# A hybrid trunk layer on one core: the plan of the engines' order takes two engines' reads of one PSUM tile as ordered

## The chip, the cores and the metric

The kernel runs on one core of a Trainium2 chip. A core has a matmul engine (PE, TensorE), a vector engine (DVE), a scalar engine (ACT), a general one (POOL) and a queue that issues DMAs (SP). Each engine takes its instructions strictly in the order in which they stand in its own queue; between engines the order is kept by semaphores. PE writes to PSUM, a small buffer that DVE and ACT read. The metric is the device time of one execution in microseconds; lower is better.

## The reference

Two layers are computed for 640 tokens (512 latent tokens and 128 context tokens). In each layer one projection of the normalised input feeds three token mixers: attention with low-rank queries and keys over 8 heads (A), a chunked DeltaNet with 4 heads in both directions (B), and a chunked gated MLP (C). Cut to what matters:

```
def _layer(x, mod, p, cache=None):
    shift, scale, gate = split(mod, 3)
    proj = (rms(x, norm_g) * (1 + scale) + shift) @ w_in
    cq, ckv, krope, z_a, qkv_b, ga, gb, z_b, cu, cv, z_c, gl = split(proj)
    o_a = attend(q, k, v)            # softmax over context and latent keys
    o_b = rms(gdn(forward) + gdn(backward))
    o_c = chunk_mlp(cu, cv)
    br = stack(o_a * silu(z_a), o_b * silu(z_b), o_c * silu(z_c))
    yb = br @ w_branch               # one matrix per branch
    y = sum(sigmoid(gl) * yb) @ w_o
    return x + gate * y

def gdn_step(S, xs):                 # one chunk of DeltaNet, one head, one direction
    v_new = u - w @ S
    o = (q * exp(g)) @ S + att @ v_new
    S = S * exp(g_last) + (k * exp(g_last - g)).T @ v_new
```

## The kernel before, in words

Activations lie with channels on partitions and the 640 tokens along the free axis, in two halves of 320 columns. A projection is a sum over 8 channel blocks, and each f32 product is made of three matmuls on parts rounded to a short form (names `hi`, `lo`, `hh`, `hl`): 24 matmuls for one half, which PE writes into a PSUM tile of the tag `dn`. PSUM has three tags with two buffers each: `dn` (dense products), `mm` (one bank) and `p2` (two banks, shown as `p` in the profile).

The kernel's body doesn't emit instructions. It calls a recorder (class `Recorder`), which keeps every operation with the tiles that it reads and writes. For each operation `add` (line 115 on) goes through the earlier accesses of its tiles and makes an earlier operation a predecessor where one of the two writes and their ranges meet. For a PSUM tile the range is the whole tile (`box`). `plan` then runs a list schedule: each operation has a cost from a table, each engine takes the ready operation of the best priority, each tile has to find a free buffer of its tag, and a hop between engines costs a fixed number of ns. `best` plans four times, with 0, 60, 120 and 180 ns added to each hop that ends on PE (`SLACKS`), and keeps the plan whose modelled total is the least. `issue` emits the instructions in the order of that plan (line 371 is the one line that emits, so nearly every row of the profile has L371), and the framework below puts in the semaphores. In the emitted program two engines never read one PSUM tile at once: the one that stands second in the order of issue waits for the first.

The places with such pairs of reads, with the names that the profile shows:

- The scan of DeltaNet (`gdn_head`, line 1018 on). For each chunk and direction PE makes two products of the state into one tile `pks` (tag `mm`). DVE makes `rp` from its left part (`Q<-mm,g_nE,G`), which the rest of the step hangs on: PE multiplies it by the inverse (`mm<-Q,G`), ACT scales the result twice (`Q<-mm,res` and `V<-mm,br`), and PE makes from it the update of the state. From the right part of `pks` the output `z` is started, on ACT for the first of the two directions that reach a chunk (`V<-mm,g_E`) and on DVE for the second. There are 32 chunk steps in all whose `z` is on ACT (4 per head, 4 heads, 2 layers). In the recorded order `rp` comes ahead of `z`.
- The MLP's normalisation (in `layer`, after `gv`): five tiles per layer of tag `dn` are read by DVE's `bn_stats` and by ACT's copy (`D<-dn`).
- The low-rank projections (`lowrank`), the heads' preparation (`prep`) and the context part of attention (`context_tile`, with two softmaxes on one tile).

The scans of heads 0 to 3 and the preparation of attention run beside dense projections that the planner lays between them; after about 40% of a layer the attention stage runs beside the projections of branches A and C, and then come the branches' and the output's dense products.

Of the kernel before, what the change touches and what calls it, by code (L numbers as in the profile page):

```python
# [59 lines left out]
class Recorder:  # L60
# [57 lines left out]
    def add(self, eng, meth, args, kw):  # L118
        op = Op()
        op.n, op.eng, op.meth, op.args, op.kw = len(self.ops), eng, meth, args, kw  # L120
        op.prio = op.n - self.off
        op.preds, op.succs, op.tiles = set(), [], []
        outs, ins = [], []
        for i, x in enumerate(args):
            if isinstance(x, bass.AP):
                (outs if i == 0 else ins).append(x)
        for k, x in kw.items():
            if isinstance(x, bass.AP):
                (outs if k == "accum_out" else ins).append(x)
        for w, aps in ((False, ins), (True, outs)):  # L130
            for ap in aps:
                nm = ap.tensor.name
                if nm not in self.tag:
                    continue
                p0, p1, m = self.box(ap)
                lst = self.acc.setdefault(nm, [])
                keep = []
                for a_ in lst:
                    q, qw, q0, q1, qm = a_
                    hit = (w or qw) and q0 < p1 and p0 < q1 and (m & qm)  # L140
                    if hit and q is not op:
                        op.preds.add(q.n)
                    if not (w and p0 <= q0 and q1 <= p1 and (qm & ~m) == 0 and q is not op and q.eng != "SP"):
                        keep.append(a_)
                keep.append((op, w, p0, p1, m))
                self.acc[nm] = keep
                u = self.users.setdefault(nm, [])
                if not u or u[-1] is not op:
                    u.append(op)
                if nm not in op.tiles:  # L150
                    op.tiles.append(nm)
        self.cost(op, outs, ins)
        self.ops.append(op)
# [1656 lines left out]
```

## Time and profile before

| | us |
|---|---|
| median of 3 runs | 1702.54 (1701.52 to 1705.32) |
| the profiled execution's own time | 1704.07 |
| its span, from the first to the last instruction | 1702.3 |
| PE busy | 1646.9 (97%) |
| DVE busy | 1287.8 (76%) |
| ACT busy | 884.9 (52%) |

The profile is of one execution, whose time is 1.5 us above the median of the runs. PE is busy nearly throughout. A layer takes about 850 us, and the second shows nearly the same pattern as the first. What is below the span is PE's idle time, and it lies in few places: the start, the stretch with the DeltaNet heads in both layers, and the border between the layers.

### The profile page before, as it was taken

The numbers are of one execution on the slowest core, as the hardware profiler recorded it, in microseconds if no ns is written. First come the engines' busy times: TensorE is split into PE (matmuls) and PEld (weight loads), VectorE is DVE, ScalarE is ACT, GpSimd is POOL, SyncE is SP. The second block draws the span as 40 slices with busy tenths as digits, with TensorE's granted clock in tenths as the row PEclk, the third lists the DMA queues.
The fourth block names the chain that finished last, engine by engine and source line by source line (L and its number), as shares of the span: only waits on it lengthen the run. The fifth ranks groups of instructions, "written<-read, shape, count | busy, mean of one in ns | idle before, by whom it ended". The sixth has DMA issues, their size and how long they took to land.

```text
span 1702.3 us, 34983 instructions
## 1 busy us (share of the span) xinstructions
PE 1646.9 (97%) x13286; PEld 1538.8 (90%) x13286; DVE 1287.8 (76%) x3638; ACT 884.9 (52%) x2201; POOL 16.6 (1%) x100
## 2 busy tenths in 40 slices
PE   6999999999999999999999999999999999999998
PEld 5998988999888889999989989889988888899998
DVE  4898888565655777887987988885656557779898
ACT  3566665554544554444445676645545445545453
POOL 0000000000000000000000000000000000000000
PEclk9999999999999999999989999999999999999999
DMA  9311211221111213564542212112221122123252
GB/s 295 99 54 51 62 57 44 70 63 59 47 58 49 84 59 107 157 201 153 189 154 59 61 42 62 57 57 64 69 59 40 53 63 74 52 83 101 85 168 80
DMA packets 94617, 146.39 MB, mean 86 GB/s; under 512 B 14064, under 2 KB 38000, under 8 KB 94448
## 3 DMA queue, kind: packets, MB, share of 16 engines
q1 hardware_dynamic: 94448, 144.15, 27.5%
q8 instruction: 105, 1.72, 0.4%
q14 instruction: 64, 0.52, 0.1%
HBM read 132.28 MB, written 11.83 MB: 85 GB/s over the span
## 4 chain that ended last, share of the span: by engine, by line
PE 84%; DVE 8%; ACT 6%; issue 1%; DMA 0%; SPq 0%; DVEq 0%; ACTq 0%
PE dn L371 44%; PE p L371 24%; PE mm L371 16%; ACT iv L371 2%; DVE lo L371 1%; DVE iv L371 1%; DVE C L371 1%; ACT G L371 1%; DVE G L371 1%; ACT hi L371 1%; DVE ya L371 1%; ACT V L371 1%; DVE mx L371 1%; ACT C L371 1%; DVE D L371 0%
## 5 line engine op out<-in xcount | busy, mean ns | idle before, releaser
L371 PE MATMUL dn<-hh,hi 128*128 128x320 f32 (+1 forms) x1472 | 469.5, 319 | 7.7 <-ACT hh L371 4.2
L371 PE MATMUL dn<-hh,lo 128*128 128x320 f32 (+1 forms) x1472 | 470.8, 320 | 0.0
L371 PE MATMUL dn<-hl,hi 128*128 128x320 f32 (+1 forms) x1472 | 468.9, 319 | 0.0
L371 PEld LDWEIGHTS dn<-hh,hi 128*128 128x128 f32 (+1 forms) x1472 | 276.9, 188 | 14.6 <-ACT hh L371 5.6
L371 PEld LDWEIGHTS dn<-hl,hi 128*128 128x128 f32 (+1 forms) x1472 | 277.5, 189 | 5.1 <-issue 2.8
L371 PEld LDWEIGHTS dn<-hh,lo 128*128 128x128 f32 (+1 forms) x1472 | 277.5, 189 | 3.6 <-issue 1.8
L371 ACT CAST hi<-raw 128x512 fp32r<-128x512 f32 (+1 forms) x300 | 185.8, 619 | 179.0 <-PE dn L371 79.1
L371 DVE TENSOR_TENSOR lo<-raw,hi 128x512 fp32r<-128x512 f32 (+1 forms) x300 | 205.7, 686 | 66.6 <-ACT hi L371 61.5
L371 PE MATMUL dn<-qkv,hi 128*128 128x320 f32 x768 | 176.4, 313 | 0.0
L371 PEld LDWEIGHTS dn<-qkv,hi 128*128 128x128 f32 x768 | 129.8, 189 | 2.5 <-ACT hi L371 1.6
L371 PE MATMUL dn<-qkv,lo 128*128 128x320 f32 x384 | 120.1, 313 | 0.0
L371 ACT CAST hi<-D 128x512 fp32r<-128x512 f32 x88 | 54.6, 621 | 108.0 <-PE dn L371 55.4
L371 PE MATMUL p<-hh,hi 128*128 128x320 f32 x296 | 92.2, 312 | 0.6 <-ACT hi L371 0.6
L371 PE MATMUL p<-hl,hi 128*128 128x320 f32 x296 | 92.2, 312 | 0.2 <-DVE hl L371 0.2
L371 PE MATMUL p<-hh,lo 128*128 128x320 f32 x296 | 92.1, 311 | 0.0
L371 DVE TENSOR_REDUCE mx<-p 128x1 f32<-128x640 f32 x64 | 52.6, 821 | 50.1 <-PE p L371 50.1
L371 ACT ACTIVATE V<-p,mx,scl 128x640 f32<-128x640 f32 x64 | 56.6, 884 | 58.2 <-DVE mx L371 53.1
L371 PEld LDWEIGHTS dn<-qkv,lo 128*128 128x128 f32 x384 | 72.7, 189 | 0.0
L371 ACT COPY V<-p 128x640 f32<-128x640 f32 x64 | 44.6, 698 | 49.3 <-PE p L371 49.1
L371 PE MATMUL p<-G,G 128*128 128x512 f32 x128 | 66.1, 598 | 4.1 <-ACT G L371 4.1
L371 PE MATMUL p<-G,hi 128*128 128x320 f32 x286 | 69.4, 308 | 0.0
L371 ACT ACTIVATE th<-dn 128x320 f32<-128x320 f32 x112 | 48.7, 435 | 39.7 <-PE dn L371 39.5
(350 smaller groups left out, 3471.7 us busy)
## 6 DMA issues: line engine op xcount, KB each, us to landing
raw<-in_w_in SPq DMA_DIRECT2D x212, 256.0 KB, 2.7
G<-in_w_mod SPq DMA_DIRECT2D x96, 256.0 KB, 4.2
raw<-in_w_branch SPq DMA_DIRECT2D x48, 256.0 KB, 2.8
D<-in_w_in SPq DMA_DIRECT2D x32, 256.0 KB, 3.4
ld<-sp SPq DMA_DIRECT2D x16, 320.0 KB, 3.1
raw<-in_w_o SPq DMA_DIRECT2D x20, 256.0 KB, 3.0
G<-in_w_uq SPq DMA_DIRECT2D x16, 192.0 KB, 2.8
D<-in_w_o SPq DMA_DIRECT2D x12, 256.0 KB, 3.9
```

The lines of the kernel that those rows point to most:

```text
L371: op.ins = getattr(getattr(nc, ENG[op.eng]), op.meth)(*op.args, **op.kw)
```

## The change

A predecessor is now also recorded between two reads of one PSUM tile if they are on different engines, in the order in which they were recorded (`self.tag[nm][1]` is true for a PSUM tile).

```diff
@@ -137,7 +137,7 @@
                 keep = []
                 for a_ in lst:
                     q, qw, q0, q1, qm = a_
-                    hit = (w or qw) and q0 < p1 and p0 < q1 and (m & qm)
+                    hit = (w or qw or (self.tag[nm][1] and q.eng != op.eng)) and q0 < p1 and p0 < q1 and (m & qm)
                     if hit and q is not op:
                         op.preds.add(q.n)
                     if not (w and p0 <= q0 and q1 <= p1 and (qm & ~m) == 0 and q is not op and q.eng != "SP"):
```

No operation is added or removed; the plan is another, and with it the order on every engine. The planner also keeps another of its four plans: the one with 60 ns added to hops that end on PE, where it kept the one with 0 before. PE's order differs in 482 places, most of them in the DeltaNet and attention stages of both layers.

On DVE, in the scan of head 0 in layer 0 (`Q_387` is `rp` of one chunk step, `mm_386` its tile; `dn_661` is the last of the five tiles of the MLP's normalisation), before:

```order
L371 BN_STATS st_594_662<-dn_661 128x6 [waits Activation_49]
L371 BN_AGGR mv_648<-st_591_659 128x2 [waits DVE_49]
L371 SCALAR_TENSOR_TENSOR Q_385<-Q_369,g_E_223,mm_384 128x128 [waits PE_49]
L371 BN_AGGR mv_648<-st_594_662 128x2 [waits DVE_49]
L371 SCALAR_TENSOR_TENSOR Q_387<-mm_386,g_nE_224,G_301 128x128 [waits Activation_49]
```

And now, on DVE:

```order
L371 SCALAR_TENSOR_TENSOR Q_385<-Q_369,g_E_223,mm_384 128x128 [waits PE_49]
L371 BN_AGGR mv_648<-st_591_659 128x2 [waits DVE_49]
L371 TENSOR_TENSOR iv_545<-iv_545,iv_542 128x10x13
L371 BN_STATS st_594_662<-dn_661 128x6 [waits PE_49]
L371 SCALAR_TENSOR_TENSOR Q_387<-mm_386,g_nE_224,G_301 128x128 [waits PE_49]
```

On ACT, the same step's `z` (`V_368<-mm_386`), before:

```order
L371 ACTIVATE V_366<-mm_382,br_226_294 128x128
L371 COPY D_663<-dn_661 128x512 [waits PE_49]
L371 ACTIVATE C_513<-C_504,l_conv_w_197 128x644 [waits Activation_49,Pool_49]
L371 ACTIVATE V_368<-mm_386,g_E_223 128x128 [waits PE_49]
L371 ACTIVATE G_518<-c_masks_71,g_gh_221 128x128 x3
```

And now, on ACT:

```order
L371 COPY D_660<-dn_658 128x512 [waits DVE_49]
L371 ACTIVATE G_518<-c_masks_71,g_gh_221 128x128 x2
L371 COPY D_663<-dn_661 128x512 [waits DVE_49]
L371 ACTIVATE V_368<-mm_386,g_E_223 128x128 [waits DVE_49]
L371 ACTIVATE G_518<-c_masks_71,g_gh_221 128x128
```

Before, DVE's `rp` waits for ACT's `z`, and `bn_stats` for ACT's copy; now ACT waits for DVE in both. Over the program `z` came first in 30 of the 32 pairs, and now in none; of the ten copies of the normalisation eight came first, and now none.

On PE, ahead of the scores of head 3 in layer 0, before (`dn_676` is the last dense tile of that head's v, `p2_679` its decays, and the `mm` products belong to the end of head 1's scan):

```order
L371 MATMUL dn_676_744<-hl7_128_196,hi_673_741 128x320
L371 MATMUL mm_566_634<-V_511_579,G_251_319 128x128
L371 MATMUL mm_566_634<-V_512_580,G_252_320 128x128
L371 MATMUL mm_567_635<-Q_561_629,qkv_187_255 128x128
L371 MATMUL mm_567_635<-Q_561_629,qkv_175_243 128x128
L371 MATMUL dn_676_744<-hh7_127_195,lo_674_742 128x320
L371 MATMUL p2_679_747<-G_680_748,c_strict_5_73 128x512
```

And now, on PE:

```order
L371 MATMUL dn_676_744<-hl7_128_196,hi_673_741 128x320
L371 MATMUL dn_676_744<-hh7_127_195,lo_674_742 128x320
L371 MATMUL p2_679_747<-G_680_748,c_strict_5_73 128x512
L371 MATMUL mm_566_634<-V_511_579,G_251_319 128x128
L371 MATMUL mm_566_634<-V_512_580,G_252_320 128x128
L371 MATMUL mm_567_635<-Q_561_629,qkv_187_255 128x128
L371 MATMUL mm_567_635<-Q_561_629,qkv_175_243 128x128
```

The dense tile is finished four small products earlier. What follows from it is head 3's convolution on DVE (`C_745`), before:

```order
L371 SCALAR_TENSOR_TENSOR C_745<-C_736,l_conv_w_197,C_745 128x644 [waits Activation_49]
L371 TENSOR_TENSOR V_581<-mm_638,V_581 128x128 [waits DVE_49,PE_49]
L371 SCALAR_TENSOR_TENSOR C_745<-C_736,l_conv_w_197,C_745 128x644 [waits DVE_49]
L371 SCALAR_TENSOR_TENSOR C_745<-C_736,l_conv_w_197,C_745 128x644 [waits DVE_49,Pool_49]
L371 SCALAR_TENSOR_TENSOR C_745<-C_736,l_conv_w_197,C_745 128x644 [waits DVE_49]
L371 SCALAR_TENSOR_TENSOR qkv_735<-C_746,C_745 128x512 [waits Activation_49]
```

And now, on DVE:

```order
L371 SCALAR_TENSOR_TENSOR C_745<-C_736,l_conv_w_197,C_745 128x644 [waits Activation_49]
L371 STREAM_TRANSPOSE iv_794<-iv_791 128x160
L371 SCALAR_TENSOR_TENSOR C_745<-C_736,l_conv_w_197,C_745 128x644 [waits DVE_49]
L371 TENSOR_TENSOR iv_796<-iv_770,c_msk_9_77 128x160
L371 TENSOR_TENSOR V_581<-mm_638,V_581 128x128 [waits PE_49]
L371 SCALAR_TENSOR_TENSOR C_745<-C_736,l_conv_w_197,C_745 128x644 [waits DVE_49,Pool_49]
L371 SCALAR_TENSOR_TENSOR C_745<-C_736,l_conv_w_197,C_745 128x644 [waits DVE_49]
L371 SCALAR_TENSOR_TENSOR qkv_735<-C_746,C_745 128x512 [waits Activation_49]
```

Two operations of head 2's inverse (`iv`) now stand between the four steps of the convolution; they stood ahead of it before.

## Rows read from the trace of the kernel before

**Rows 1.** The page: span, and busy time of PE.

```profile
span 1702.3 us, 34983 instructions
PE 1646.9 (97%) x13286; PEld 1538.8 (90%) x13286; DVE 1287.8 (76%) x3638; ACT 884.9 (52%) x2201; POOL 16.6 (1%) x100
```

**Rows 2.** Busy time of each engine in stretches, then granted clock, DMA.

```profile
core 0: us, PE busy (x) PEld busy (x) DVE busy (x) ACT busy (x) POOL busy (x), PEclk, DMA share, GB/s
0.00:50.00 50.00, 34.66 (x381) 27.36 (x382) 25.39 (x70) 17.00 (x28) 0.71 (x13) 0.97 0.87 272
...
140.00:350.00 210.00, 198.47 (x2048) 184.96 (x2047) 164.47 (x599) 127.47 (x396) 5.26 (x21) 0.98 0.19 56
350.00:650.00 300.00, 296.08 (x2151) 268.68 (x2150) 192.66 (x539) 151.20 (x350) 0.00 (x0) 0.99 0.22 65
650.00:840.00 190.00, 190.00 (x1386) 180.02 (x1386) 158.16 (x314) 83.94 (x153) 0.00 (x0) 1.00 0.51 164
...
990.00:1200.00 210.00, 198.76 (x2019) 185.69 (x2020) 164.04 (x599) 125.75 (x390) 5.26 (x21) 0.98 0.19 56
1200.00:1500.00 300.00, 296.07 (x2147) 268.73 (x2146) 191.75 (x535) 151.80 (x353) 0.00 (x0) 0.99 0.21 62
```

**Rows 3.** PE's timeline: start, duration, instruction, [idle before it <- releaser].

```profile
145.02 0.84 PE L371 MATMUL p<-iv,iv 32*32 32x32 f32 x60 [2.34 <-ACT iv L371]
...
157.96 0.65 PE L371 MATMUL dn<-c_ident,ya 128*128 128x128 f32 x4 [0.62 <-ACT D L371]
...
249.55 2.50 PE L371 MATMUL p<-qkv,qkv 128*128 128x128 f32 x10 [3.54 <-ACT junk L371]
...
283.39 0.49 PE L371 MATMUL mm<-Q,G 128*128 128x128 f32 x2 [0.24 <-ACT Q L371]
...
1096.48 2.50 PE L371 MATMUL p<-qkv,qkv 128*128 128x128 f32 x10 [3.54 <-ACT junk L371]
```

**Rows 4.** Granted clock in two stretches behind long waits; columns as in rows 2.

```profile
146.00:150.00 4.00, 3.90 (x16) 3.72 (x16) 3.83 (x10) 1.26 (x4) 0.17 (x3) 0.57 0.06 22
250.00:255.00 5.00, 5.00 (x19) 3.97 (x19) 4.16 (x32) 1.95 (x12) 0.00 (x0) 0.50 0.01 3
```

**Rows 5.** Timeline of one chunk step of the scan.

```profile
281.64 0.37 ACT L371 ACTIVATE V<-mm,g_E 128x128 f32<-128x128 f32 x1 [0.93 <-PE mm L371]
...
282.04 0.35 DVE L371 SCALAR_TENSOR_TENSOR Q<-mm,g_nE,G 128x128 f32<-128x128 f32 x1
```

**Rows 6.** PE's waits in total: waited for, us, times, longest.

```profile
PE mm L371 <- ACT Q L371: 1.5, 4, 0.5
```

**Rows 7.** Timeline ahead of the scores of head 3.

```profile
237.08 0.34 DVE L371 STREAM_TRANSPOSE iv<-iv 128x160 f32<-128x160 f32 x1
...
238.62 0.32 DVE L371 TENSOR_TENSOR iv<-iv,c_msk 128x160 f32<-128x160 f32 x1
...
241.68 0.61 PE L371 MATMUL mm<-V,G 128*128 128x128 f32 x4
...
241.88 0.62 ACT L371 CAST hi<-raw 128x512 fp32r<-128x512 f32 x1 [0.52 <-PE dn L371]
...
242.49 0.40 PE L371 MATMUL dn<-hh,lo 128*128 128x320 f32 x1
...
242.92 0.49 ACT L371 COPY C<-dn 128x192 f32<-128x192 f32 x2 [0.42 <-PE dn L371]
...
248.21 0.74 ACT L371 ACTIVATE C<-C 128x644 f32<-128x644 f32 x1 [0.42 <-DVE C L371]
248.86 0.29 ACT L371 ACTIVATE Q<-V 128x128 f32<-128x128 f32 x1
...
249.15 0.26 ACT L371 ACTIVATE junk<-p 128x128 f32<-128x128 f32 x1
```

**Rows 8.** Timeline of one context softmax of attention.

```profile
432.97 0.45 ACT L371 ACTIVATE iv<-mm,mx,scl 128x128 f32<-128x128 f32 x1
...
435.06 0.28 DVE L371 TENSOR_SCALAR iv<-iv,ls 128x128 f32<-128x128 f32 x1
```

## The prediction

> **What bounds the kernel now.** I read the page's busy times first: PE works 1646.9 of 1702.3 us [rows 1]. No instruction is added or removed, so the change can only give or take idle time of PE, 55.4 us in all, and time at which PE's clock is low. The second view, the windows by stage, says where the idle time lies [rows 2]: 15.3 us at the start (50.00 less 34.66), 11.5 in the DeltaNet stretch of layer 0 (210.00 less 198.47) and 11.2 in that of layer 1, 3.9 in each attention stretch, and nothing in 650 to 840. In the dense stretch PE runs 1386 matmuls in 190 us, 0.137 us each, and no order of its queue changes that. So about 30 us, in the DeltaNet and attention stretches, are open to this change. The third view, PE's own timeline there, gives each wait and its releaser [rows 3]: two waits of a layer are long (2.34 us on ACT in head 0's inverse, 3.54 us on ACT's squares ahead of head 3's scores), and the others, some twenty in a layer, last 0.15 to 1.05 us each. The layers agree: the 3.54 us stand in both.
>
> **The change part by part.**
>
> *The scan.* In the chunk step shown, ACT starts `z` at 281.64 and ends at 282.01, and DVE's `rp` starts at 282.04 [rows 5]: the reader that nobody hurries for goes first and the chain loses 0.40 us. In 30 of 32 steps this is turned round, so 30 times the chain gets 0.40 us shorter. Of these 12 us only what PE waits for counts. PE waits for the scan's ACT results four times, 1.5 us in all [rows 6]; one of them is the 0.24 us at 283.39, in the very step shown [rows 3]. All four end on a result that `rp` leads to, and none is longer than 0.5, so 0.40 off the chain removes nearly all of it. I take -1.5 us; the ends are 0 (PE's queue is moved by as much) and -1.5. What then comes late is `z`, by 0.35, the length of DVE's `rp` [rows 5]; it is needed when the second direction reaches the chunk, later in the scan, and that hides it. If it were not hidden, the same four waits would be back at about 0.35, 1.4 us.
>
> *The MLP's normalisation.* DVE's statistics now come ahead of ACT's copy in all ten tiles. PE waits 0.62 us for ACT's copy once a layer [rows 3], because the `dn` tile is free only after both readers. Two readers one after the other need the same sum either way round; only the plan's knowledge of it is new, and PE's order has more dense products between these transposes. I take half of 2 x 0.62: -0.6 us, between 0 and -1.2.
>
> *The long wait of head 0's inverse.* ACT's list ahead of the awaited copy holds the same operations as before, so the 2.34 us stay, in both layers.
>
> *The long wait ahead of head 3's scores.* Here the chain is: PE ends head 3's last dense tile, ACT copies it out (242.92, after 0.42 of waiting for PE), DVE does four steps of the convolution, ACT's tanh starts at 248.21 after 0.42 of waiting for DVE, and behind it in ACT's queue stand one square of the norm (0.29) and the last square that frees PE's buffer (249.15) [rows 7]. Two things move. The dense tile ends earlier: four small products (two rows of 0.61 us that overlap, 241.68 to 242.49) come behind its last matmul, 0.8 us, but ACT's cast from 241.88 to 242.50 keeps the copy from gaining more than 0.4 [rows 7]. And two operations of head 2's inverse now stand between the convolution's steps on DVE: 0.34 and 0.32 us, which overlap a little with their neighbours, so 0.6 [rows 7]. One more short ACT operation also stands ahead of the convolution; the nearest row is the square of 0.29. Net: +0.6 + 0.3 - 0.4 = +0.5 us a layer, +1.0 in both. Ends: -0.4 a layer if the added operations fit into waits, +0.9 if the copy gains nothing.
>
> *The context softmax.* Its two softmaxes share a tile, so DVE's second maximum now waits for ACT's first exponential, which stood directly ahead of the second one (432.97) before; the second now has to wait for one DVE step and its hops. The first exponential is 0.45 long [rows 8], so I estimate 0.5 to 1.0 us. The scaling that PE waits for ran at 435.06, over 1.6 us after the second exponential's end at 433.42, because DVE was busy with a query tile: that hides it. I take 0; without that cover it would be at most 8 x 1.0 = +8 us for the four head pairs and two layers. ACT stands still meanwhile, and behind it are casts for the dense products; ACT is busy 151 of 300 us there [rows 2], so it catches up.
>
> *Low-rank projections and head preparation.* One more change of engine per tile; the tile is needed again only after 24 dense matmuls at 0.137, 3.3 us. I take 0.
>
> *The other added delay.* With 60 ns on each hop to PE in the plan, dependent products stand later in PE's queue: head 2's first scan product comes 12 matmuls later in the order, its last 17 later, and the lag is gone before attention starts. That can shorten the remaining short waits (at most 0.06 for each of some 36, -2.2 us) or let the scan run out of cover. I take 0 and keep both for the range.
>
> *Sum.* -1.5 - 0.6 + 1.0 = -1.1 us against the profiled execution's 1704.07 (span 1702.3 and 1.8 around it): 1703.0. That execution is 1.5 above the median of the runs, so the same difference from 1702.54 gives **1701.4 us**. A measurement of this kernel can tell 0.2%, 3.4 us, from no change, so this is no change.
>
> **The rivals.**
>
> *Nothing that PE feels.* The emitted program kept the two readers apart before, so only the order of the two is new, and PE's dense work covers both. For it: nothing idles in 650 to 840, and 12 us of chain stand against 1.5 us of waits [rows 2, 6]. Against it: those 1.5 us. Time: 1702.5.
>
> *A truer plan closes the short waits everywhere.* A plan that knows of the reads puts PE's dependent products where they are ready. The idle time of a layer's two stretches is 15.4 us [rows 2]; without the two long waits (5.9) and the two terms above (0.75 and 0.62) 8.1 are left, 16 in both layers. If half of that goes, -8, and with the scan's and the normalisation's -2.1 the time is 1692.4. Against it: many of these waits (for casts, for the query tile) have no double read in front of them.
>
> *A long wait grows or a new one opens: slower.* One mechanism: the scan of heads 2 and 3 stands 12 to 17 matmuls (about 2 us at 0.137) later against the dense products, which end where they did; where the dense products of a stage run out, ahead of head 3's scores and at the next inverse, PE meets a chain that is 2 us late and waits for it. It decides if the lag isn't gone by then. Behind the two long waits the granted clock was 0.57 for 4 us and 0.50 for 5 us [rows 4], the lower of the two levels (1.2 against 2.4 GHz) for most of both stretches, where it was 1.00 in 650 to 840 [rows 2]; so a wait of over 2 us costs its length and about 0.43 x 4 = 1.7 us more. Price: (2.0 + 1.7) in each layer, +7.4: 1709.9. The Trainium skill (TensorE: Matmul & The Clock Gate, Part 1) says the same of idle time: the array falls to half rate after it and gets its full clock back only after sustained work; that page would have the 1.7 paid for each new long wait, and a reading without it would give 1706.5. Against the rival: PE reaches head 3's scores after as many matmuls as before (1618 in both orders), so the lag isn't there yet at the place where cover is known to be short.
>
> **How the numbers follow.** My forecast 0.40, the first rival 0.15, the truer plan 0.25, the slower case 0.20. The forecast's own range is 1698 to 1705: -2.2 from the added delay and the better ends of the normalisation and of the wait ahead of head 3 on one side, +0.8 and part of the context's 8 on the other. A fifth of it, 0.08 of 0.40, lies below 1699.1 (0.2% under the median), hardly any above 1705.9. So faster 0.33, same 0.47, slower 0.20. The range that should hold 8 times in 10 reaches to the prices of the two rivals that move the time, 1692 to 1710; about half of each lies beyond, 0.12 and 0.10.
>
> **What the profile of the changed kernel would show.** Right: in each scan step DVE's `rp` starts with PE's result and ACT's `z` behind it; no PE wait for ACT in `mm<-Q,G` above 0.2; the wait for ACT's normalisation copy gone or halved; the wait ahead of head 3's scores 3.5 to 4.5; busy time of PE as before; the idle time of 140 to 350 at 11 us or little less. Wrong: a new PE wait above 1.5 us in heads 2 or 3 or in attention, with the clock at 0.5 behind it, or an idle time of the two stretches below 11 us a layer, where it was 15.

## The result

The changed kernel takes 1680.63 us (median; 1678.77 to 1684.49) against 1702.87 us for the kernel before on the same chip: a ratio of 0.9871, interval 0.9850 to 0.9891, so 22 us faster. The forecast was 1701.4, in a range of 1692 to 1710. The profiled execution of after took 1684.49 (span 1682.7), that of before 1704.07 (span 1702.3): 19.6 us between the spans. The profiled execution of after is the slowest of its four.

### The profile page after: what moved, and what is told of

Read it like the earlier page. It is cut to its first block, busy times and chain, and to the rows that moved or that the text cites. A ratio compares the mean times of both kernels' runs of the same rounds, so it can differ in the third digit from the quotient of the medians.

```text
span 1682.7 us, 34992 instructions
## 1 busy us (share of the span) xinstructions
PE 1634.6 (97%) x13286; PEld 1535.0 (91%) x13286; DVE 1286.6 (76%) x3638; ACT 887.4 (53%) x2201; POOL 16.7 (1%) x100
## 5 line engine op out<-in xcount | busy, mean ns | idle before, releaser
L371 DVE TENSOR_REDUCE mx<-p 128x1 f32<-128x640 f32 x64 | 52.7, 823 | 48.2 <-PE p L371 48.1
L371 PEld LDWEIGHTS p<-iv,G 32*32 32x32 f32 (+2 forms) x608 | 34.9, 132 | 35.7 <-issue 32.9
```

Of the source, the lines that this page charges most:

```text
L371: op.ins = getattr(getattr(nc, ENG[op.eng]), op.meth)(*op.args, **op.kw)
```

## The profile after

The first lines of the page of after, span and busy times, answer to [rows 1]:

```profile
span 1682.7 us, 34992 instructions
...
PE 1634.6 (97%) x13286; PEld 1535.0 (91%) x13286; DVE 1286.6 (76%) x3638; ACT 887.4 (53%) x2201; POOL 16.7 (1%) x100
```

The same 13286 matmuls count 12.3 us less busy time (1646.9 to 1634.6), and PE's idle time falls by 7.3 (55.4 to 48.1). The forecast held that the first of these would stay. The larger part of the gain lies there; at most 3.4 of the 12.3 us are clock (last section).

The windows of after, with the columns of [rows 2]:

```profile
140.00:350.00 210.00, 199.92 (x2045) 188.74 (x2044) 166.51 (x605) 127.27 (x395) 5.32 (x21) 0.98 0.20 58
350.00:650.00 300.00, 299.96 (x2199) 275.34 (x2198) 196.98 (x546) 156.25 (x355) 0.00 (x0) 1.00 0.22 66
...
990.00:1200.00 210.00, 202.19 (x1995) 192.35 (x1996) 166.09 (x606) 128.33 (x400) 5.15 (x18) 0.98 0.20 58
1200.00:1500.00 300.00, 299.40 (x2190) 274.71 (x2190) 198.04 (x545) 153.23 (x341) 0.00 (x0) 1.00 0.22 64
```

The stretches are the same in time, not in work, since after runs ahead of before in them (its first exponential of the latent keys comes 7.1 us earlier). In these 300 us of attention PE now runs 2199 matmuls instead of 2151 [rows 2]. Its idle time there fell by only 3.9 us, to 0.04. Its weight loads (PEld) grew by 6.7 us of busy time (268.68 to 275.34). Over the whole span PEld's time without work fell from 163.5 to 147.7 us, 15.8 of the 19.6, where PE's own idle time shows 7.3.

The Trainium skill (Perfetto Trace Analysis, Identifying the Most-Contended Engine) warns of this: the matmul row's busy share is a bad measure of headroom, because matmuls are pipelined, and the share of peak FLOPs and the busy share of the weight loads are to be used instead. The trace agrees as far as it goes: PEld rose from 90.4% to 91.2% of the span, PE by half as much, from 96.7% to 97.1%.

PE's long waits in the timeline of after (start, duration, instruction, [idle before it <- releaser]) answer to [rows 3]:

```profile
142.56 0.84 PE L371 MATMUL p<-iv,iv 32*32 32x32 f32 x60 [2.05 <-ACT iv L371]
...
155.46 0.66 PE L371 MATMUL dn<-c_ident,ya 128*128 128x128 f32 x4 [0.16 <-ACT D L371]
...
244.31 1.01 PE L371 MATMUL p<-qkv,qkv 128*128 128x128 f32 x3 [3.35 <-ACT junk L371]
...
1083.56 2.50 PE L371 MATMUL p<-qkv,qkv 128*128 128x128 f32 x10 [3.36 <-ACT junk L371]
```

The two long waits of layer 0 stand almost as they were (2.34 to 2.05, 3.54 to 3.35), and no new one came. The gain is in neither of them.

## The place the forecast passed over

The preparation of the next head pair's queries runs beside the softmax of the present one. Its product tile `pq` takes two PSUM banks and has three readers: VectorE's multiplication, and two squares on ScalarE.

```
V.scalar_tensor_tensor(n2(qT), h2(pq), qcol[:, 0:1], n2(ropeT), ALU.mult, ALU.mult)
S.activation(n2(sq[0][up]), h2(pq)[0:64], AF.Square)
S.activation(n2(sq[1][r0]), h2(pq)[64:96], AF.Square)
```

Before, the plan let the squares run beside VectorE's read, and the finished program did not. One of the three places of layer 0 where this reaches PE, in the timeline of before:

```profile
418.87 0.89 ACT L371 ACTIVATE V<-p,mx,scl 128x640 f32<-128x640 f32 x1 [3.05 <-DVE mx L371]
...
420.55 0.88 DVE L371 SCALAR_TENSOR_TENSOR G<-p,l_q_col,c_ropeT 128x640 f32<-128x640 f32 x1
...
421.46 1.41 ACT L371 ACTIVATE G<-p 64x640 f32<-64x640 f32 x2 [1.61 <-DVE G L371]
421.66 0.31 PE L371 MATMUL dn<-hh,hi 128*128 128x320 f32 x1
421.80 0.31 PE L371 MATMUL dn<-hl,hi 128*128 128x320 f32 x1
421.95 0.30 PE L371 MATMUL dn<-hh,lo 128*128 128x320 f32 x1
422.92 1.13 PE L371 MATMUL p<-G,G 128*128 128x512 f32 x2 [0.67 <-ACT G L371]
```

VectorE reads the tile from 420.55. ScalarE stands still for 1.61 us behind it, and its two squares end at 422.87. Only then is the tile free for PE's next scores (`p<-G,G`), which start at 422.92. PE takes its queue in order, and these scores stand next in it.

The rows also show how much of such a wait the busy time swallows. Dense matmuls start 0.147 us apart and each counts 0.31 busy, so the last one covers 0.16 of the wait. From 421.95 to 422.92 are 0.97 us, of which 0.67 is shown as idle. By these numbers a wait of less than 0.16 behind a dense matmul isn't shown at all.

The Trainium skill (PSUM — Partial Sum Buffer, PSUM bank collisions raise a hardware error) says that the compiler's scheduler sets one behind the other any two accesses by different engines to one bank and quadrant, reads and writes alike. The rows agree: VectorE's read ends at 421.43, and ScalarE's first square starts at 421.46.

The same place in the timeline of after:

```profile
414.30 1.41 ACT L371 ACTIVATE G<-p 64x640 f32<-64x640 f32 x2 [1.61 <-DVE G L371]
...
415.53 0.31 PE L371 MATMUL dn<-hh,hi 128*128 128x320 f32 x1
415.67 0.31 PE L371 MATMUL dn<-hl,hi 128*128 128x320 f32 x1
415.82 0.64 PE L371 MATMUL p<-G,G 128*128 128x512 f32 x1
```

ScalarE waits as long as before, 1.61. PE doesn't: the plan knows when the tile comes free and has put ten dense products between the transposes and the scores where five stood before, and the scores start 0.15 after the last one.

Over the whole program, first the waits of PE for these squares and then the squares themselves (idle time before them behind the bar), before:

```profile
PE p L371 <- ACT G L371: 4.1, 6, 0.7
```

```profile
L371 ACT ACTIVATE G<-p 64x640 f32<-64x640 f32 x16 | 11.2, 697 | 16.0 <-DVE G L371 13.9 <-PE p L371 1.9
L371 ACT ACTIVATE G<-p 32x640 f32<-32x640 f32 x16 | 11.1, 696 | 7.7 <-DVE G L371 7.6
```

And after:

```profile
PE p L371 <- ACT G L371: 0.6, 1, 0.6
```

```profile
L371 ACT ACTIVATE G<-p 64x640 f32<-64x640 f32 x16 | 11.2, 700 | 10.6 <-DVE G L371 10.6
L371 ACT ACTIVATE G<-p 32x640 f32<-32x640 f32 x16 | 11.2, 699 | 0.2
```

The second square's own 7.7 us of waiting are gone. In before, some tiles were read by ScalarE, then by VectorE, then by ScalarE again, with a wait at each turn. Now both squares stand behind VectorE's read. ScalarE's idle time ahead of the squares falls from 23.7 to 10.8 us.

## The experiments

All 18 were run beside the kernel before. Behind each stand its median in us and its ratio to before with the 95% interval. The planner chose slack 0 in before and slack 60 in after; each run below fixes one.

### Slack or the new orders?

Before with slack 60, after with slack 0, after with 120, before with 120:

```diff
-SLACKS = (0, 60, 120, 180)
+SLACKS = (60,)
```

> The kernel before with one edit: the planner may only use the plan with 60 ns added to hops that end on PE (before, it kept the one with 0). No predecessor between reads. Theory A (the reads' predecessors make the gain: the plan no longer places dependent products too early): 1699 to 1706, as before. Theory B (the other slack makes the gain, the predecessors only tipped the choice): 1678 to 1686.

> The changed kernel with the planner held to the plan with 0 ns added, as the kernel before. Theory A (the predecessors make the gain): 1678 to 1686. Theory B (the slack makes it): 1699 to 1706. If both count: between, and this run's gain and the one of the kernel before with 60 ns add up to about 22 us.

> The changed kernel with the planner held to 120 ns. Theory A: the slack moves little, within 5 us of the changed kernel, 1676 to 1686. Theory B: more slack keeps helping or turns round; below 1678 or above 1690.

> The kernel before with the planner held to 120 ns, no predecessor between reads. Theory A: 1697 to 1707. Theory B: within 5 us of the kernel before with 60 ns, so 1676 to 1690.

Before with slack 60: 1695.92, 0.9947 (0.9932 to 0.9962). After with slack 0: 1680.05, 0.9849 (0.9828 to 0.9870). After with 120: 1691.11, 0.9925 (0.9909 to 0.9942). Before with 120: 1696.66, 0.9958 (0.9945 to 0.9972). The new orders make the gain without any slack. Slack alone gives 7 to 9 us with the old rule, adds nothing at 60 with the new one, and at 120 loses 11 of the gain. Only after with slack 0 lies where theory A put it; the other three miss its ranges by 0.3 to 5 us, so the slack isn't without effect. At 120 most of that goes with the granted clock (last section).

### The direction of the scan's reads

First, the old plan and the same rows on every queue, with only the wait between the scan's two readers turned round after planning, so that `z` waits for `rp`. Second, the new rule for the scan's pair alone. Third, the new rule for all but that pair. Fourth, the new rule with `z` recorded ahead of `rp`.

```diff
+ zs = [x for x in u if x.eng == "S" and "V" in tagof(x)]
+ rs = [x for x in u if x.eng == "V" and "Q" in tagof(x) and x.n < (zs[0].n if zs else 0)]
...
+ out.pop(j)
+ out.insert(i, r)
```

```diff
-(self.tag[nm][1] and q.eng != op.eng)
+(self.tag[nm][0] == "mm" and q.eng == "V" and op.eng == "S" and op.kw is not None and self.tag[args[0].tensor.name][0] == "V")
```

```diff
-(self.tag[nm][1] and q.eng != op.eng)
+(self.tag[nm][1] and q.eng != op.eng and not (self.tag[nm][0] == "mm" and q.eng == "V" and op.eng == "S" and op.kw is not None and self.tag[args[0].tensor.name][0] == "V"))
```

```diff
-V.scalar_tensor_tensor(rp, pks[:, 0:P], nE[:, d, t, col : col + 1], vt[:, t, :], ALU.mult, ALU.add)
 if zdone[t] == 0:
     S.activation(z[:, t, :], pks[:, P : 2 * P], AF.Copy, scale=E[:, d, t, col : col + 1])
+V.scalar_tensor_tensor(rp, pks[:, 0:P], nE[:, d, t, col : col + 1], vt[:, t, :], ALU.mult, ALU.add)
```

> The kernel before with every engine's own queue exactly as it was; in the 30 scan steps in which DVE's rp waited for ACT's z, ACT's z now waits for DVE's rp. Theory C (the wait's direction makes the gain: the scan's chain gets 0.40 us shorter 30 times, and PE's dependent products wait less): 1680 to 1693. Theory D (the plan's knowledge makes it: queues laid out for the true times): 1700 to 1705, and at worst 1708.

> Slack 0; the predecessor is recorded only between rp and z of the scan (32 pairs), for no other read. If the scan is the cause of the 23 us: 1678 to 1686. If the other reads (attention's preparation, context softmax, low-rank projections, normalisation) are: 1697 to 1705.

> Slack 0; predecessors between all reads by two engines except rp and z of the scan. If the scan is the cause: 1697 to 1706. If the other reads are: 1678 to 1688. If both add up, this run's gain and that of the run with the scan alone make 23 us together.

> Slack 0; all predecessors as in the changed kernel, but z is recorded ahead of rp where it is on ACT, so that the plan knows of the wait and rp waits for z in all 32 steps. Theory C (direction): the scan's share of the gain is lost, 1692 to 1703. Theory D (knowledge): 1678 to 1688.

Turned waits alone: 1705.05, 1.0018 (1.0004 to 1.0032), slower by 0.7 to 5.4 us. Scan pair alone: 1704.61, 1.0005 (0.9990 to 1.0019). All but the scan: 1685.15, 0.9901 (0.9876 to 0.9926). `z` first but known: 1682.17, 0.9882 (0.9860 to 0.9905).

That the waits were really turned is seen in the run with turned waits alone (who waited for whom, us, times, longest). PE's waits for the scan's results:

```profile
PE mm L395 <- ACT Q L395: 2.3, 5, 0.6
```

and ScalarE's for `rp`:

```profile
ACT V L395 <- DVE Q L395: 38.1, 32, 2.0
```

and the latter before:

```profile
ACT V L371 <- DVE Q L371: 5.9, 6, 1.4
```

PE's waits stayed: 2.3 us in five there, 1.5 in four before [rows 6]. So the direction of these waits brings nothing with the old plan, and with `z` first but known 20 of the 26 us (by the ratios) that the new rule gives at slack 0 stay. The reads outside the scan carry 17 of the 26. In the run with turned waits ScalarE waited 32 us more for `rp` and 16 less for PE's products, and the time grew by 3 only, so ScalarE's idle time by itself isn't the price of an order.

### Which of the other reads?

The new rule at slack 0, for one kind of tile at a time: the 512-wide product tiles without the scan, the dense tiles, the two-bank tiles; and of the first kind the context softmax alone. The edits, one of the four new lines in each (`scan pair` is the condition shown above):

```diff
-(self.tag[nm][1] and q.eng != op.eng)
+(self.tag[nm][0] == "mm" and q.eng != op.eng and not (scan pair))
+(self.tag[nm][0] == "dn" and q.eng != op.eng)
+(self.tag[nm][0] == "p2" and q.eng != op.eng)
+(self.tag[nm][0] == "mm" and q.eng != op.eng and "mx1" in (self.tag[q.args[0].tensor.name][0], self.tag[args[0].tensor.name][0]))
```

> The changed planner rule at slack 0, only for readers of the 512-wide product tiles, the scan's reads left out: that is keys, values and queries of the attention's prep where two engines read one tile, and the context softmax (maximum by VectorE, exponential by ScalarE). All the other places keep the kernel before's rule. All other reads together gave 17.4 us (1702.5 to 1685.2). Theory A1 (one kind of place carries it, and it lies in the attention stretch, where the landmarks gain 5 us a layer): 1687 to 1692. Theory A2 (each place has its share, the sum over the three kinds is 17): 1694 to 1699. Theory A3 (any other plan falls elsewhere by chance, no place carries it): anything between 1685 and 1705, and the three parts don't add up to 17.

> The rule at slack 0 only for readers of the dense products' tiles: high and low parts, squares and copies of the low-rank products, statistics and copy of the scan's norm. A1: no gain, 1700 to 1704, since the attention's softmax keeps the old plan. A2: 1694 to 1699, part of the gain before the attention stretch. A3: anything from 1685 to 1705.

> The rule at slack 0 only for readers of the two-bank tiles: scores of the latent softmax (maximum by VectorE, exponentials by ScalarE) and the turned queries of the prep. A1: if these carry it 1687 to 1692, then the 512-wide tiles give nothing. A2: 1694 to 1699. A3: anything from 1685 to 1705.

> The rule at slack 0 only where one of the two readers is the maximum of the context softmax, on 512-wide tiles: 8 softmaxes a layer pair, nothing else. If the context softmax carries what the 512-wide tiles give, within 2 us of that run; if prep carries it, 1700 to 1704. By A3 it has a time of its own with no relation to the run of the 512-wide tiles, though the changed edges are a part of that run's.

512-wide tiles: 1698.14, 0.9972 (0.9954 to 0.9989). Dense tiles: 1702.77, 0.9998 (0.9982 to 1.0014). Two-bank tiles: 1689.66, 0.9928 (0.9906 to 0.9949). Context softmax alone: 1700.72, 0.9990 (0.9974 to 1.0007).

The three kinds come to -4.8, -0.3 and -12.3 us, together the 17 of the run with all but the scan, which speaks against theory A3. One kind of place, the two-bank tiles, carries most of it. On the two-bank tiles the maximum and the exponential of a softmax were ordered already, by the data that go from one to the other. The orders that are new there are 32: the two squares of 16 query tiles behind VectorE's read.

### Those orders, or another plan's luck?

A plan differs in thousands of rows as soon as one number changes. So the complement was run (the rule for all but the two-bank tiles), and the planner's cost of every product's end was made 10 ns longer, with the old rule and with the new one. The fourth run is after with slack 30.

```diff
-(self.tag[nm][1] and q.eng != op.eng)
+(self.tag[nm][1] and q.eng != op.eng and self.tag[nm][0] != "p2")
```

```diff
-op.lat = op.occ + 180
+op.lat = op.occ + 190
```

> The new rule at slack 0 for all tiles but the two-bank ones (so the squares of the queries are planned beside VectorE's read again, as before). Theory P (the 32 orders on the queries' tiles carry 12 us): 1680 plus 12, so 1690 to 1694. Rival L (luck of the plan): no relation, anywhere from 1680 to 1705.

> The kernel before at slack 0 with 10 ns more on the end of every product in the planner's costs: a plan that differs in thousands of rows, with nothing known that was unknown. P: within 3 us of before, 1699 to 1706. L: a scatter as large as the gain, that is 1680 to 1700 is as likely as not.

> The changed kernel at slack 0 with the same 10 ns. P: within 4 us of 1680, 1676 to 1684. L: 1685 to 1705.

> The changed kernel with slack 30, between the two that gave 1680.0 (0) and 1680.6 (60). P: 1677 to 1684. L: anything up to 1705. If it is under 1679 it is the best version here.

All but the two-bank tiles: 1695.78, 0.9949 (0.9934 to 0.9963), so these tiles are worth 17 us when the others are known (0.9949 less 0.9849), more than the 12 alone, and the time is 2 us above what theory P allowed. Old rule with the 10 ns: 1699.44, 0.9970 (0.9959 to 0.9981). New rule with them: 1680.87, 0.9864 (0.9847 to 0.9881). After with slack 30: 1678.15, 0.9848 (0.9833 to 0.9863).

The 10 ns moved the old rule's time by 5 us, outside what was expected of them: a plan's luck is worth about that much, and some 2 of the 5 go with the granted clock (last section). The gain of the 512-wide tiles, 4.8, can't be told from it. The 12 to 17 us of the two-bank tiles can. Slack 30 has the lowest median, but its interval overlaps that of the changed kernel, so it isn't shown to be better.

### Cover moved to the place by hand

The old plan. At the six places (three a layer) where scores wait for a query tile, the next seven dense products of PE's queue are set ahead of the scores; nothing else is moved. (`op` is the first matmul of the scores, `cand` the seven products.)

```diff
 out = self.best()
...
+for x in cand:
+    out.remove(x)
+i = out.index(op)
+out[i:i] = cand
```

> The kernel before with its own plan; after planning, at the six places (three a layer) where the scores of a tile wait for the two-bank tile that the squares of the next pair's queries hold, the next seven dense products of TensorE's queue are set ahead of the scores. All other queues and TensorE's queue elsewhere are the kernel before's. Theory W (the wait at these places is the cost): the steps in front of these scores, 0.96 to 1.05 us, shrink to about 0.15, six times 0.84 is 5 us, so 1697 to 1699. If the later waits of the same tile (transposes 0.46, context softmax's second transposes 0.56) fall with it, up to 9 us, 1693 to 1696. Rival (the place is hidden anyway, the gain is made elsewhere in the new plan): 1701 to 1704.

1701.23, 0.9999 (0.9986 to 1.0011): nothing. The timeline of this run at the place shown above (its lines have another number, since the file is longer):

```profile
414.53 0.89 ACT L405 ACTIVATE V<-p,mx,scl 128x640 f32<-128x640 f32 x1 [2.93 <-DVE mx L405]
...
418.63 0.31 PE L405 MATMUL dn<-hh,hi 128*128 128x320 f32 x1
418.78 1.02 PE L405 MATMUL p<-G,G 128*128 128x512 f32 x2
...
423.76 0.41 PE L405 MATMUL p<-c_ident,V 128*128 128x128 f32 x2 [1.09 <-DVE V L405]
...
432.81 0.89 ACT L405 ACTIVATE V<-p,mx,scl 128x640 f32<-128x640 f32 x1 [0.33 <-DVE mx L405]
```

The wait ahead of the scores is gone, and the transposes behind them wait 1.09 us instead. The seven products were their cover. From the exponential at 414.53 to the one at 432.81 are 18.28 us. In before, from 418.87 to 437.15, they are 18.28 as well:

```profile
437.15 0.89 ACT L371 ACTIVATE V<-p,mx,scl 128x640 f32<-128x640 f32 x1 [0.33 <-DVE mx L371]
```

So cover taken from the next wait gains nothing. The theory that the wait of these scores alone is the cost fell.

### The unplanned order itself taken away

The old plan and the same rows on all queues, with the squares reading a constant table in SBUF, so that the queries' sums of squares are left out:

```diff
 S.activation(n2(sq[0][up]), h2(pq)[0:64], AF.Square)
+rec.ops[-1].args = (rec.ops[-1].args[0], n2(ropeT)[0:64], AF.Square)
 S.activation(n2(sq[1][r0]), h2(pq)[64:96], AF.Square)
+rec.ops[-1].args = (rec.ops[-1].args[0], n2(ropeT)[64:96], AF.Square)
```

> The kernel before with its own plan and the same rows on every queue; only the two squares of each query tile read a constant table in SBUF instead of the product tile (so the sums of squares of the queries are left out). Then nothing orders them behind VectorE's read, as the old plan believes, and the scores at the six places no longer wait for ScalarE. Theory O (the unplanned order itself is the cost): the steps ahead of the six scores shrink by 0.84 each, 5 us, and up to 9 with the later waits of the same softmax: 1694 to 1698. Theory L (it costs nothing, since the next wait on the softmax's chain takes over as in the run before): 1701 to 1704. If the whole 12 us of the two-bank orders hang on it: 1690 to 1692.

1688.98, 0.9912 (0.9898 to 0.9925): 15 us faster (12.8 to 17.4), 1 us below the lowest range expected. The timeline at the same place:

```profile
413.87 0.89 ACT L371 ACTIVATE V<-p,mx,scl 128x640 f32<-128x640 f32 x1 [3.07 <-DVE mx L371]
...
416.95 0.31 PE L371 MATMUL dn<-hh,lo 128*128 128x320 f32 x1
417.10 1.02 PE L371 MATMUL p<-G,G 128*128 128x512 f32 x2
...
430.34 0.89 ACT L371 ACTIVATE V<-p,mx,scl 128x640 f32<-128x640 f32 x1
```

With the same PE queue the scores follow 0.15 after the dense product. The softmax behind them starts earlier too, and so the stretch between the two exponentials takes 16.47 us instead of 18.28. Measured so at each of the six places, the trace gives 4.9 us in layer 0 and 5.0 in layer 1.

PE's queue is the same in both runs, so the traces can also be laid over each other matmul by matmul. That shows two more places, one a layer, ahead of the first scores. In before, in layer 0:

```profile
367.65 0.70 ACT L371 ACTIVATE G<-p 64x640 f32<-64x640 f32 x1 [1.47 <-DVE G L371]
...
371.20 0.30 PE L371 MATMUL dn<-hh,hi 128*128 128x320 f32 x1
372.21 1.01 PE L371 MATMUL p<-D,G 128*128 128x320 f32 x5 [0.71 <-DVE G L371]
```

and in this run:

```profile
367.18 0.31 PE L371 MATMUL dn<-hh,hi 128*128 128x320 f32 x1
367.33 0.90 PE L371 MATMUL p<-D,G 128*128 128x320 f32 x5
```

The square waits 1.47 us for VectorE, what stands behind it on ScalarE and then on VectorE comes late, and PE waits for that. PE's step shrinks from 1.01 to 0.15, and the lead of this run grows by 1.0 us there, in each layer. So 12 of the 15 us are shown at eight places. The other 3 aren't located, and the clock isn't it (last section).

The edit takes more away than the order behind VectorE: the squares no longer wait for PE's product either. That share is small. At the place of the 1.61 us the tile's last product ends at 420.08, 0.23 us into the wait, and of the 23.7 us over the program 1.9 are put down to PE.

The squares, as groups of this run, no longer wait:

```profile
L371 ACT ACTIVATE G<-c_ropeT 32x640 f32<-32x640 f32 x16 | 11.8, 736 | 0.2
L371 ACT ACTIVATE G<-c_ropeT 64x640 f32<-64x640 f32 x16 | 11.7, 732 | 0.2
```

This shows the cause of the larger part of the gain. The old plan was good for a program in which the squares don't wait for VectorE, and about 15 us were lost because the finished program made them wait: ScalarE idled 23.7 us ahead of them (16.0 and 7.7 above), in the middle of the chain from one softmax to the next. The changed rule doesn't remove the order; it plans with it.

## Why the prediction was wrong

- **Head preparation.** This step failed, and it is the largest. It was taken as 0, because "the tile is needed again only after 24 dense matmuls". For the dense tiles the run with them alone shows no gain. For the query tiles the count was wrong: at the place shown only eleven dense matmuls and five transposes stood between the tile's last product and the scores that take its place, while VectorE's read and the two squares took until 422.87. The orders on these tiles measured -12 alone and -17 beside the others, and the squares without the unplanned order -15. The rows for it were there to be read: 23.7 us of idle time ahead of the squares, 21.5 of them behind VectorE, and six waits of PE for them. The "query tile" that the forecast took as cover for the context softmax is one of these reads.
- **PE's busy time.** The change was to "only give or take idle time of PE" and time at a low clock, so that about 30 us were open, and busy time was to stay as before. This step failed too. Busy time covers 0.16 us of every wait behind a dense matmul, and 12.3 of the 19.6 us show as less busy time, at most 3.4 of them clock. Counted from the trace, the steps from the start of a dense matmul to that of a smaller product over 0.4 us at full clock were 30 in before, 24.1 us in all, and 12 in after, 10.7 us.
- **The scan.** Taken as -1.5. The direction alone gave +3 (interval +0.7 to +5.4), the scan's orders alone +0.9 (-1.7 to +3.2). PE's four waits for the scan's results, 1.5 us, are gone in after as forecast, but that alone gains nothing. Beside the others the scan's orders are worth 9 us (0.9901 to 0.9849), about 3 of them clock (last section). Why only there isn't settled; up to 5 of it may be a plan's luck.
- **The normalisation.** The wait fell from 0.62 to 0.16 in each layer, near the better end of the term, but the run with the dense tiles alone shows no gain in time (-3.1 to +2.4).
- **The long waits.** Right that both stay. The one ahead of head 3's scores was to grow by 0.5 a layer, and shrank by 0.2.
- **The context softmax.** Taken as 0, with up to +8 if the cover failed. Its run gave -1.7 (-4.4 to +1.2), which can't be told from 0.
- **The slack.** Taken as 0, right for the changed kernel: 0, 30 and 60 all lie at 1678 to 1681.
- **The rivals.** The truer plan that closes the short waits was the right mechanism, at a chance of 0.25, and 12 us too small, since its price was half of the idle time that PE's row shows. Even all 16 us of it and the two terms would have fallen short of the 22. No new long wait opened, so the slower rival fell. One sign of being wrong came: the idle time of the two stretches fell below 11 us a layer, to 10.1 and 8.4.

## What to carry to other kernels

A planner must know every order that the finished program will have, reads against reads in PSUM among them. Look for such orders on the engine that waits, not on the one that is busy: group ScalarE's and VectorE's idle time by releaser, and ask which of those waits the plan doesn't know. Don't read the room for a better order from the matmul row's idle time: take start-to-start steps, or the weight loads' busy time. And a wait isn't closed with cover that the next wait needs. Before a few microseconds are put down to a plan, the granted clocks of the runs belong beside them.

## What the runs showed of the hardware

PE's granted clock is part of the difference between the two profiled executions. In the windows of before, a stretch in which PE is busy throughout:

```profile
378.00:382.00 4.00, 4.00 (x19) 4.00 (x18) 3.21 (x11) 2.88 (x5) 0.00 (x0) 0.57 0.00 1
```

About the same part of the work in after:

```profile
371.00:375.00 4.00, 4.00 (x30) 4.00 (x29) 3.94 (x20) 2.69 (x5) 0.00 (x0) 1.00 0.08 9
```

0.57 is the lower of the two levels (1.2 against 2.4 GHz) for most of the stretch. Ahead of it PE had waited 0.71 us (at 372.21, above) and had run twenty products one column wide (375.00 to 377.31). That alone doesn't decide it: the run with seven products ahead has such a wait (0.72 us) and the same twenty products, and the clock stays at 1.00 there; the run with the squares elsewhere has no such wait, and it falls. What sets a fall off wasn't tried.

All stretches at the lower level add to 44.4 us in the profiled execution of before and 37.5 in that of after. At half speed that is at most 3.4 us of the 19.6. They differ between plans and executions: 32.7 us in the run with the squares elsewhere and 30.7 in the one with seven products ahead, of which only the first is faster.

The mean granted clock of nearly every execution is on record, so its part can be estimated. Over the 96 executions of before that ran beside the experiments, 0.001 more of it goes with 0.7 to 1.2 us less time (the slope within each of the six groups that ran together). The four executions of after have 0.9905 on average, those 96 of before 0.9897: about 1 us of the 22. The run with the squares elsewhere has 0.9894 and before beside it 0.9896, the two-bank tiles 0.9903 and 0.9904, so none of their 15 and 12 us is clock. But before with slack 120 has 0.9936 against 0.9884, which is about 5 of its 7 us, and after with slack 120 has 0.9842 where it has 0.9918 with slack 0, about 7 of the 11 that are lost. Of the scan's 9 us beside the others it is about 3, since the mean was 0.0034 above before's with the scan's orders and 0.0004 without them, and of the 5 us that the 10 ns gave about 2 (0.9902 against 0.9884).
